# A hybrid attention and convolution layer on one core: low score products on half the array's rows, low weights last, and a new order

## The chip, the cores and the metric

The kernel runs on one core of a Trainium2 chip. The metric is the device time of one execution in microseconds (us). Of the kernel before, three runs were timed: a median of 910.27 us (909.42 to 910.80). One further execution was recorded by the profiler.

## What is computed

One layer on 1024 positions of width 1024: an RMS norm, one input projection to 5632 columns, then two branches, attention over 16 heads of 64 (4 key and value heads) in three dilations and a causal convolution of 31 taps, both gated; an output projection, a residual and a last RMS norm. Cut to what matters here:

```python
h = rmsnorm(x, norm_g[layer])
proj = jnp.einsum('bsd,de->bse', h, w_in[layer])
q, k, v, a_gate, c_val, c_glu, c_gate = jnp.split(proj, split_idx, axis=-1)
y_att = attention_branch(q, k, v, a_gate)      # scores: einsum of q and k per block, softmax, times v
y_conv = conv_branch(c_val, c_glu, c_gate, conv_w[layer], ...)
y = jnp.concatenate([y_att, y_conv], axis=-1)
x = x + jnp.einsum('bse,ed->bsd', y, w_out[layer])
```

All of it is float32.

## The kernel before

**Numbers in two parts.** TensorE takes float32r operands, so a float32 number is split into a high part (its rounding to float32r) and a low part (what is left). A projection then is three products: high weight by high input, high weight by low input, low weight by high input. In the input projection (`inproj`, L640) a column of 128 outputs over 512 positions is 8 chunks of the width times these three, 24 products of 512 columns into one bank of PSUM. The tiles are `wh` and `wl` (weights), `hhi` and `hlo` (input), `ps` (result). The raw weight comes by a DMA of SP (`raw`); ScalarE writes `wh` and a negated copy, and a DMA of GpSimd's queue adds `raw` to the copy, which makes `wl` (`split_dma`). The first two weights are split by ScalarE and VectorE without that DMA.

**Scores.** Heads work in pairs (`attend`, L793). The 128 rows of a head's query tile hold the high part in one half of the rows and the low part in the other; for the first head of a pair (j = 0) the high part is in rows 0 to 63, for the second in rows 64 to 127. A key tile `kdh` holds the high part of the keys in both halves, `kdl` the low part in both. One product of 128 rows with `kdh` thus gives (high + low query) by high key, and a second one with `kdl` adds (high + low query) by low key. For each pair there are 32 such couples of products, called units: 16 far ones (8 of 96 columns, 8 of 224, tiles `qf`, `sc_..far`) and 16 near ones (2 of 128, 14 of 256, tiles `qs`, `sc_..near`). `score` (L830) writes the products of two or four units into one of two banks `sc`, then VectorE reads each unit with an add and a minimum (`add_min`, L283), and ScalarE takes the exponential. The transposes `tp_*`, the products `on`, `of` with the values and the additions follow.

**The order.** Nothing is issued in the order in which it is written. Every operation is recorded with a cost in microseconds, and `Plan.order` makes one list by simulating the engines: it picks ready operations by priority, keeps the number of buffers of a kind within `LIMITS`, and takes the streams of work from `SECTIONS` (which projections stand beside which pair of heads: h convolution input, k, q, v, a and c gates). `TUNE` holds the priorities. `mm` (L216) gives the cost of products. Each engine then executes its part of the list strictly in that order, waiting where data are late.

Of the kernel before, what the change touches and what calls it, by code (L numbers as in the profile page):

```python
# [19 lines left out]
ND = D // P  # L20
# [14 lines left out]
LIMITS = {"x": 5, "raw": 2, "raw_oc": 1, "raw_oa": 2, "wh": 3, "wl": 3, "tab": 1, "e": 7, "pt": 4, "vs": 4, "vc":  # L35
          4, "turn": 2, "opsa": 2, "score": 2, "hc": 5, "c": 7, "t": 1, "g": 1, "gl": 7, "y": 2, "ag": 4, "cc": 5,
          "qs": 5, "qf": 4, "kdh": 9, "kdl": 5, "yc": 1, "ya": 2, "zc": 7, "za": 3}
# [6 lines left out]
TUNE = {"w": 225, "use": 260, "ln": 65, "att": 240, "conv": -15, "wo": 185, "woa": 20, "ap": 0, "wait": 0.2116}  # L44
SECTIONS = [("k0 q0 h1 v", 0), ("h2 a0 q1", 1), ("h3 a1 q2", 1), ("a2 q3 h4", 1), ("h5 k1 a3 q4", 1), ("h6 a4 q5",
            1), ("c0 h7 a5 q6 c1 q7", 1), ("a6 a7 c2 c3", 1), ("c4 c5", 1), ("c6 c7", 0)]
# [115 lines left out]
class Plan:  # L162
# [57 lines left out]
    def mm(self, calls):  # L220
# [3 lines left out]
        for out, a, b, start, stop in calls:  # L224
            outs.append(out)
            ins += [a, b]
            n = b.cols if start is not None else P
            slow = 4.0 if start is not None and b.buf.dtype == F32 else 1.0
            cost += max(n * slow / 2210.0, 0.06 if start is not None else 0.109)
# [233 lines left out]
def layer_kernel(tc, x, norm_g, w_in, conv_w, conv_b, ln_g, ln_b, w_out, fin_g, tab, out):  # L463
# [176 lines left out]
    def inproj(col, use, cuts=((0, 512), (0, 512))):  # L640
        wh, wl = load_w(col)
        for half in range(2):
            b = bank("mm", f"ps{col}_{half}")
            for n0, n1 in zip(cuts[half], cuts[half][1:]):
                if n0:
                    yield 0.5
                for c in range(ND):
                    pl.mm([(b[:, n0:n1], wh[:, c, :], hhi[half][:, c, n0:n1], c == 0, False),
                           (b[:, n0:n1], wh[:, c, :], hlo[half][:, c, n0:n1], False, False),
                           (b[:, n0:n1], wl[:, c, :], hhi[half][:, c, n0:n1], False, c == ND - 1)])  # L650
# [142 lines left out]
    def attend(p):  # L793
# [36 lines left out]
        def score(name, units):  # L830
            sc = bank("sc", f"sc{p}_{name}", "score")
            calls, outs, o = [], [], 0
            for q, keys, t, e, s, near in units:
                dst = sc[:, o:o + e.cols]
                to = dst.crossed() if near else dst
                calls += [(to, q, keys(kh), True, False), (to, q, keys(kl), False, True)]
                outs.append(dst)
                o += e.cols
            pl.mm(calls)
            for (q, keys, t, e, s, near), dst in zip(units, outs):  # L840
# [3 lines left out]
        for j in range(2):  # L844
            score(f"{j}far0", [far_unit(j, r, 0) for r in range(4)])
            for r in (0, 2):
                score(f"{j}far{r + 1}", [far_unit(j, r, 1), far_unit(j, r + 1, 1)])
            yield 3.0
# [4 lines left out]
        for j in range(2):  # L853
            for b in (0, 2, 4, 6):
# [304 lines left out]
```

## Time and profile before

| | |
|---|---|
| median of three runs | 910.27 us |
| profiled execution | 910.03 us |
| its span, first to last instruction | 908.2 us |
| TensorE products (PE) | 875.1 us busy, 4493 instructions |
| weight loads (PEld) | 731.2 us |
| VectorE (DVE) | 656.1 us |
| ScalarE (ACT) | 591.3 us |
| mean granted TensorE clock | 0.984 |

The span lies 1.8 us under the profiled execution's own time. Busy times of PE are those of a pipeline: one product's latency is counted, and products overlap, so the distance between two starts tells what a product costs. The trace of the profiled execution is asked by groups, by stretches and as a timeline.

### The profile page before, as it was taken

Reading aid. Unit: us, or ns where it says so; the run is one execution under the profiler, and the core shown is the slowest. Engines: PE = TensorE matmul, PEld = TensorE weight load, DVE = VectorE, ACT = ScalarE, POOL = GpSimd, SP = SyncE. Lnnn points to the kernel's source line nnn. Section 1 sums busy time; section 2 is a strip of 40 time slices with the busy share of each in tenths; the row PEclk is TensorE's granted clock in tenths of the full one; section 3 lists DMA queues with packets and bytes.
Section 4 is the critical chain, followed back from the end, with each engine's and each line's share of the span. In section 5 each row is a group of like instructions: output and inputs, shape, how many; then the busy total and the mean of one; then the engine's idle time right before and its main releaser. Section 6 shows DMA issues by size and latency. Waiting matters only on the chain. (4 is left out here: it accounts for less than half of the span.)

```text
span 908.2 us, 13036 instructions
## 1 busy us (share of the span) xinstructions
PE 875.1 (96%) x4493; PEld 731.2 (81%) x4493; DVE 656.1 (72%) x1506; ACT 591.3 (65%) x1392; POOL 53.3 (6%) x69
## 2 busy tenths in 40 slices
PE   8999999999999999999998998899999899999996
PEld 7888888878888888878886887688887678778885
DVE  5769995798699699989587658874659895615432
ACT  5777469387979889678786764795796754404111
POOL 0011001101010110100011000001000000000000
PEclk9999999999999999999999999699999999999999
DMA  7653306436353673464357323366765697758211
GB/s 259 186 119 67 96 3 140 93 91 144 70 118 59 163 165 83 93 135 101 96 128 173 70 70 92 73 152 132 206 201 194 186 372 255 252 177 239 93 47 47
DMA packets 104953, 123.53 MB, mean 136 GB/s; under 512 B 17941, under 2 KB 78357, under 8 KB 104888
## 3 DMA queue, kind: packets, MB, share of 16 engines
q1 hardware_dynamic: 97000, 94.40, 33.6%
q0 software_dynamic: 7888, 28.32, 17.2%
q8 instruction: 35, 0.57, 0.3%
q14 instruction: 30, 0.25, 0.1%
HBM read 65.35 MB, written 24.84 MB: 99 GB/s over the span
## 5 line engine op out<-in xcount | busy, mean ns | idle before, releaser
L236 PE MATMUL ps<-hhi,wh 128*128 128x512 f32 (+1 forms) x720 | 291.1, 404 | 0.2 <-ACT hhi L249 0.2
L236 PE MATMUL ps<-hhi,wl 128*128 128x512 f32 (+1 forms) x720 | 282.3, 392 | 6.1 <-DMA wl<-raw 4.8
L236 PE MATMUL ps<-hlo,wh 128*128 128x512 f32 (+1 forms) x720 | 281.8, 391 | 0.4 <-DVE hlo L264 0.3
L236 PEld LDWEIGHTS ps<-hhi,wl 128*128 128x128 f32 x720 | 136.6, 190 | 38.2 <-DMA wl<-raw 6.5
L236 PEld LDWEIGHTS ps<-hlo,wh 128*128 128x128 f32 x720 | 137.2, 191 | 23.8 <-DVE hlo L264 1.0
L236 PEld LDWEIGHTS ps<-hhi,wh 128*128 128x128 f32 x720 | 137.0, 190 | 23.0 <-issue 0.5
L251 ACT ACTIVATE e<-e,near 128x256 f32<-128x256 f32 (+1 forms) x256 | 115.0, 489 | 17.4 <-DVE near L264 11.5
L268 DVE SCALAR_TENSOR_TENSOR c<-t,taps,c 128x511 f32<-128x511 f32 (+14 forms) x120 | 88.5, 737 | 0.0
L268 DVE SCALAR_TENSOR_TENSOR c<-hc,taps,c 128x511 f32<-128x511 f32 (+14 forms) x120 | 88.2, 735 | 0.3
L268 DVE SCALAR_TENSOR_TENSOR t<-hc,taps,t 128x511 f32<-128x511 f32 (+6 forms) x112 | 82.6, 738 | 0.3 <-ACT t L251 0.2
L236 PE MATMUL opsc<-woc,yhc 128*128 128x512 f32 (+1 forms) x272 | 81.0, 381 | 0.0
L251 ACT ACTIVATE e<-e,far 128x96 f32<-128x96 f32 (+1 forms) x128 | 53.8, 423 | 25.9 <-DVE far L283 25.2
L297 POOL DMA_DIRECT2D wl<-raw x40 | 34.9, 873 | 414.2 <-ACT wl L251 315.5
L236 PEld LDWEIGHTS opsc<-woc,yhc 128*128 128x128 f32 x272 | 50.1, 188 | 10.7
L236 PE MATMUL opsc<-woc,ylc 128*128 128x512 f32 (+1 forms) x136 | 52.0, 383 | 1.4 <-DVE ylc L264 1.4
L251 ACT ACTIVATE fjunk<-zc 128x512 bf16<-128x512 f32 (+1 forms) x17 | 10.3, 606 | 62.2 <-DVE zc L264 62.2
L236 PE MATMUL opsa<-woah,yla 128*128 128x512 f32 x112 | 45.0, 402 | 2.6 <-DVE yla L264 2.6
L249 ACT CAST wh<-raw 128x1024 fp32r<-128x1024 f32 x44 | 46.0, 1046 | 0.4 <-DMA raw<-in_w_in 0.4
L236 PE MATMUL opsa<-woah,yha 128*128 128x512 f32 x112 | 45.6, 408 | 0.4 <-DVE cc L264 0.4
L236 PE MATMUL opsa<-woal,yha 128*128 128x512 f32 x112 | 45.1, 402 | 0.0
L251 ACT ACTIVATE e<-e,f 128x224 f32<-128x224 f32 (+1 forms) x128 | 45.0, 436 | 0.0
L249 ACT CAST qf<-qs 128x512 fp32r<-128x512 f32 x32 | 34.3, 1120 | 13.5 <-DVE qs L268 13.5
(176 smaller groups left out, 1525.2 us busy)
## 6 DMA issues: line engine op xcount, KB each, us to landing
raw<-in_w_in SPq DMA_DIRECT2D x44, 512.0 KB, 5.4
wl<-raw POOLq DMA_DIRECT2D x40, 512.0 KB, 4.7
x<-in_x SPq DMA_DIRECT2D x8, 512.0 KB, 10.2
tab<-in_tab SPq DMA_DIRECT2D x8, 512.0 KB, 3.8
c_dram<-c SPq DMA_DIRECT2D x8, 512.0 KB, 2.7
g_dram<-g SPq DMA_DIRECT2D x8, 512.0 KB, 3.1
raw_oa<-in_w_out SPq DMA_DIRECT2D x8, 512.0 KB, 5.1
raw_oc<-in_w_out SPq DMA_DIRECT2D x8, 512.0 KB, 7.9
```

The source lines that it names most:

```text
L236: nc.tensor.matmul(out.ap(), a.ap(), b.ap(), start=start, stop=stop)
L249: nc.scalar.copy(out.ap(), x.ap())
L251: nc.scalar.activation(out.ap(), x.ap(), func, **{k: ap_of(v) for k, v in kw.items()})
L268: lambda: self.nc.vector.scalar_tensor_tensor(out.ap(), a.ap(), ap_of(s), b.ap(), op0, op1),
L297: self.op("POOL", 1.0, lambda: self.nc.gpsimd.dma_start(ap_of(dst), x.ap(), accum_op=ALU.add), [dst], [x, dst])
```

## The change

It does four things.

1. `score` now takes both heads of a pair in one call and fills both `sc` banks. First come the products with `kdh` over 128 rows for both heads, then those with `kdl`, which read only the 64 rows with the high part of the query, the heads in turn. The product of low query by low key is left out by that.
2. In `inproj` the 16 products with `wh` come first, then the 8 with `wl`.
3. The planner counts a product of 64 rows at half its cost.
4. `LIMITS`, `TUNE` and `SECTIONS` have other values, so the whole order is made anew. The number of products is the same.

```diff
@@ -32,18 +32,18 @@
 
 
 
-LIMITS = {"x": 5, "raw": 2, "raw_oc": 1, "raw_oa": 2, "wh": 3, "wl": 3, "tab": 1, "e": 7, "pt": 4, "vs": 4, "vc":
+LIMITS = {"x": 5, "raw": 1, "raw_oc": 1, "raw_oa": 2, "wh": 3, "wl": 3, "tab": 2, "e": 7, "pt": 4, "vs": 4, "vc":
           4, "turn": 2, "opsa": 2, "score": 2, "hc": 5, "c": 7, "t": 1, "g": 1, "gl": 7, "y": 2, "ag": 4, "cc": 5,
-          "qs": 5, "qf": 4, "kdh": 9, "kdl": 5, "yc": 1, "ya": 2, "zc": 7, "za": 3}
+          "qs": 5, "qf": 4, "kdh": 9, "kdl": 6, "yc": 2, "ya": 2, "zc": 7, "za": 3}
 
 RESERVE = {"e": 7, "pt": 3}
 BANKS = {"mm": 3, "sc": 2, "tp": 2, "o": 1}
 WARM = 55
 LATE = C_CG + 6 * P
 MORE = (10, 12)
-TUNE = {"w": 225, "use": 260, "ln": 65, "att": 240, "conv": -15, "wo": 185, "woa": 20, "ap": 0, "wait": 0.2116}
-SECTIONS = [("k0 q0 h1 v", 0), ("h2 a0 q1", 1), ("h3 a1 q2", 1), ("a2 q3 h4", 1), ("h5 k1 a3 q4", 1), ("h6 a4 q5",
-            1), ("c0 h7 a5 q6 c1 q7", 1), ("a6 a7 c2 c3", 1), ("c4 c5", 1), ("c6 c7", 0)]
+TUNE = {"w": 195, "use": 240, "ln": 65, "att": 240, "conv": 5, "wo": 215, "woa": -20, "ap": 0, "wait": 0.2116}
+SECTIONS = [("k0 q0 h1 v", 0), ("h2 a0 q1", 1), ("h3 a1 q2 a2", 1), ("q3 h4", 1), ("h5 k1 a3 q4", 1), ("h6 a4 q5",
+            1), ("c0 h7 a5 q6", 1), ("c1 q7 a6 a7 c2 c3", 1), ("c4 c5", 1), ("c6 c7", 0)]
 
 
 def score_tables():
@@ -226,7 +226,8 @@
             ins += [a, b]
             n = b.cols if start is not None else P
             slow = 4.0 if start is not None and b.buf.dtype == F32 else 1.0
-            cost += max(n * slow / 2210.0, 0.06 if start is not None else 0.109)
+
+            cost += max(n * slow / 2210.0, 0.06 if start is not None else 0.109) * (0.5 if a.hi - a.lo == DH else 1.0)
 
         def fn():
             for out, a, b, start, stop in calls:
@@ -646,8 +647,10 @@
                     yield 0.5
                 for c in range(ND):
                     pl.mm([(b[:, n0:n1], wh[:, c, :], hhi[half][:, c, n0:n1], c == 0, False),
-                           (b[:, n0:n1], wh[:, c, :], hlo[half][:, c, n0:n1], False, False),
-                           (b[:, n0:n1], wl[:, c, :], hhi[half][:, c, n0:n1], False, c == ND - 1)])
+                           (b[:, n0:n1], wh[:, c, :], hlo[half][:, c, n0:n1], False, False)])
+                for c in range(0, ND, 2):
+                    pl.mm([(b[:, n0:n1], wl[:, c + i, :], hhi[half][:, c + i, n0:n1], False, c + i == ND - 1)
+                           for i in range(2)])
             pl.boost = TUNE["use"]
             use(half, b, slice(half * 512, half * 512 + 512))
             pl.boost = 0
@@ -828,32 +831,35 @@
                     sf[:, r, :, 2 * j + half:2 * j + half + 1], False)
 
         def score(name, units):
-            sc = bank("sc", f"sc{p}_{name}", "score")
-            calls, outs, o = [], [], 0
-            for q, keys, t, e, s, near in units:
-                dst = sc[:, o:o + e.cols]
-                to = dst.crossed() if near else dst
-                calls += [(to, q, keys(kh), True, False), (to, q, keys(kl), False, True)]
-                outs.append(dst)
-                o += e.cols
-            pl.mm(calls)
-            for (q, keys, t, e, s, near), dst in zip(units, outs):
+
+
+            first, second, todo = [], [[], []], []
+            for j in range(2):
+                sc, o = bank("sc", f"sc{p}_{name}_{j}", "score"), 0
+                for q, keys, t, e, s, near in units[j]:
+                    dst = sc[:, o:o + e.cols]
+                    to, r = dst.crossed() if near else dst, slice(j * DH, j * DH + DH)
+                    first.append((to, q, keys(kh), not o, False))
+                    second[j].append((to, q[r], keys(kl)[r], False, len(second[j]) == len(units[j]) - 1))
+                    todo.append((e, dst, t, s))
+                    o += e.cols
+            pl.mm(first + [c for both in zip(*second) for c in both])
+            for e, dst, t, s in todo:
                 pl.add_min(e, dst, t, 3e38, s[:, 0])
                 pl.act(e, e, AF.Exp, bias=s[:, 0], scale=-1.0, accum=s[:, 1])
 
-        for j in range(2):
-            score(f"{j}far0", [far_unit(j, r, 0) for r in range(4)])
-            for r in (0, 2):
-                score(f"{j}far{r + 1}", [far_unit(j, r, 1), far_unit(j, r + 1, 1)])
-            yield 3.0
+        score("far0", [[far_unit(j, r, 0) for r in range(4)] for j in range(2)])
+        yield 3.0
+        for r in (0, 2):
+            score(f"far{r + 1}", [[far_unit(j, r, 1), far_unit(j, r + 1, 1)] for j in range(2)])
+            yield 2.0
         there, back = (dram([512, n], f"{x}{p}") for x, n in (("there", 8), ("back", 4)))
         near_rows, far_rows = ("(b p) x -> p b x", dict(p=P)), ("(u r) x -> u r x", dict(r=4))
         pl.store(there.rows(far_rows[0], **far_rows[1]), sf.shaped("p a b c -> p a (b c)", 4, 8))
         pl.load(st[:, :, 1, :, :].shaped("p a b c -> p a (b c)", 4, 8), there.rows(near_rows[0], **near_rows[1]))
-        for j in range(2):
-            for b in (0, 2, 4, 6):
-                score(f"{j}near{b}", [near_unit(j, b), near_unit(j, b + 1)])
-                yield 1.0
+        for b in (0, 2, 4, 6):
+            score(f"near{b}", [[near_unit(j, b), near_unit(j, b + 1)] for j in range(2)])
+            yield 2.0
         w = pl.buf("sx", [P, 4, 2, 2, 4], F32, f"w{p}")
         f = pl.buf("sx", [P, 4, 2, 4], F32, f"f{p}")
         least, low = w[:, :, 0, 0, :], [st[:, :, k, 0, :] for k in range(2)]
```

The order on TensorE (PE), at the scores of the last but one pair of heads (`sc6`; 0 and 1 are its heads in `sc6_1far0` and `sc6_far3_0`, the number behind far or near is the block; `ps896` is the projection of the last pair's queries, `ps4736` one of the convolution gates). Before:

```order
L236 MATMUL ps896_1_5562<-hhi1_424,wh896_5265 128x512
L236 MATMUL ps896_1_5562<-hlo1_439,wh896_5265 128x512
L236 MATMUL ps896_1_5562<-hhi1_424,wl896_5275 128x512
L236 MATMUL sc6_1far0_5613<-kdh3_3677,qf13_5355 128x96
L236 MATMUL sc6_1far0_5613<-kdl3_3703,qf13_5355 128x96
...
L236 MATMUL sc6_1far1_5622<-kdh3_3677,qf13_5355 128x224
L236 MATMUL sc6_1far1_5622<-kdl3_3703,qf13_5355 128x224
...
L236 MATMUL sc6_1far3_5634<-kdh3_3677,qf13_5355 128x224
L236 MATMUL sc6_1far3_5634<-kdl3_3703,qf13_5355 128x224
...
L236 MATMUL sc6_0near0_5647<-kdh3_3677,qs12_5318 128x128
L236 MATMUL sc6_0near0_5647<-kdl3_3703,qs12_5318 128x128
```

Now, at the same pair:

```order
L237 MATMUL ps4736_1_5500<-hhi1_420,wh4736_5272 128x512
L237 MATMUL ps4736_1_5500<-hlo1_430,wh4736_5272 128x512
L237 MATMUL ps4736_1_5500<-hhi1_420,wl4736_5284 128x512 x6
L237 MATMUL sc6_far3_0_5559<-kdh3_3578,qf12_5410 128x224 x2
L237 MATMUL sc6_far3_1_5560<-kdh3_3578,qf13_5416 128x224 x2
L237 MATMUL sc6_far3_0_5559<-kdl3_3598,qf12_5410 128x224
L237 MATMUL sc6_far3_1_5560<-kdl3_3598,qf13_5416 128x224
...
L237 MATMUL ps4736_1_5500<-hhi1_420,wl4736_5284 128x512 x2
L237 MATMUL ps896_0_5575<-hhi0_232,wh896_5455 128x512
L237 MATMUL ps896_0_5575<-hlo0_236,wh896_5455 128x512
...
L237 MATMUL sc6_near0_0_5598<-kdh3_3578,qs12_5394 128x128
```

Before, the three products of a chunk stand together, and the groups of scores of this pair follow one another; now the low weights are at the end of a half projection, both heads' low products alternate, and projection products stand between any two groups of scores (8 at least, in 22 of 56 cases exactly 8, in 11 more about 10).

The order on SP, at the start of the program (`raw3584` and `raw2560` are the first two weights, `raw1024` and `raw0` the next). Before:

```order
L294 DMA raw3584_164<-in_w_in 128x8x128
L294 DMA x2_166<-in_x 128x1024
L294 DMA x3_168<-in_x 128x1024
L294 DMA raw2560_170<-in_w_in 128x8x128
L294 DMA x4_172<-in_x 128x1024
...
L294 DMA raw1024_264<-in_w_in 128x8x128
L294 DMA rows_177<-in_conv_b 1x1024
L294 DMA raw0_273<-in_w_in 128x8x128
L294 DMA rows_177<-in_ln_b 1x1024
L294 DMA x7_321<-in_x 128x1024
```

Now:

```order
L295 DMA raw3584_164<-in_w_in 128x8x128
L295 DMA x2_166<-in_x 128x1024
L295 DMA x3_168<-in_x 128x1024
L295 DMA x4_170<-in_x 128x1024
...
L295 DMA rows_172<-in_conv_b 1x1024
L295 DMA rows_172<-in_ln_b 1x1024
L295 DMA raw2560_273<-in_w_in 128x8x128
L295 DMA x7_322<-in_x 128x1024
L295 DMA raw1024_339<-in_w_in 128x8x128
```

The second weight has moved from SP's 7th transfer to its 14th, behind the two row loads; the third and fourth follow it.

## Rows read from the trace of the kernel before

**Rows 1.** The page: its head, and each engine's busy us, share and instructions.
```profile
span 908.2 us, 13036 instructions
...
PE 875.1 (96%) x4493; PEld 731.2 (81%) x4493; DVE 656.1 (72%) x1506; ACT 591.3 (65%) x1392; POOL 53.3 (6%) x69
```

**Rows 2.** TensorE's groups by form: shapes, count | busy us, mean ns | idle before, releaser.
```profile
L236 PE MATMUL ps<-hhi,wl 128*128 128x512 f32 x688 | 272.5, 396 | 4.8 <-DMA wl<-raw 4.8
...
L236 PE MATMUL ps<-hhi,wl 128*128 128x256 f32 x32 | 9.8, 306 | 1.3 <-DVE wl L264 1.3
```

**Rows 3.** Timeline of TensorE, a near group: start us, us, what, [idle before <-releaser].
```profile
117.29 0.28 PE L236 MATMUL sc_0near<-kdl,qs 128*128 128x256 f32 x1
117.41 0.28 PE L236 MATMUL sc_0near<-kdh,qs 128*128 128x256 f32 x1
```

**Rows 4.** Timeline of the weight loads (PEld) in a far group of 96 columns.
```profile
70.03 0.19 PEld L236 LDWEIGHTS sc_0far<-kdh,qf 128*128 128x128 f32 x1
70.14 0.19 PEld L236 LDWEIGHTS sc_0far<-kdl,qf 128*128 128x128 f32 x1
```

**Rows 5.** Timeline of TensorE around the products of 34 rows.
```profile
25.89 0.38 PE L234 MATMUL xT<-ident,x 128*128 128x128 f32 x2
...
26.20 0.68 PE L234 MATMUL par_ps<-ident,rows 34*128 34x34 f32 x8
...
26.66 0.22 PE L234 MATMUL par_ps<-ident,rows 34*128 34x34 f32 x1
26.82 0.38 PE L236 MATMUL ps<-hhi,wh 128*128 128x256 f32 x1
27.04 0.28 PE L236 MATMUL ps<-hlo,wh 128*128 128x256 f32 x1
```

**Rows 6.** Timeline of TensorE at its longest wait for a low weight.
```profile
487.65 0.39 PE L236 MATMUL ps<-hhi,wh 128*128 128x512 f32 x1
487.88 0.40 PE L236 MATMUL ps<-hlo,wh 128*128 128x512 f32 x1
492.34 0.50 PE L236 MATMUL ps<-hhi,wl 128*128 128x512 f32 x1 [4.06 <-DMA wl<-raw]
```

**Rows 7.** Stretches: length, busy us (count) of PE, PEld, DVE, ACT, POOL, clock, DMA, GB/s.
```profile
493.00:496.40 3.40, 3.40 (x10) 2.66 (x9) 0.99 (x2) 0.00 (x0) 0.00 (x0) 0.50 1.10 209
568.10:581.70 13.60, 9.86 (x34) 8.22 (x35) 10.94 (x45) 11.10 (x39) 0.89 (x1) 0.50 0.48 113
```

**Rows 8.** Timeline of TensorE at a bunch of score products.
```profile
564.26 0.27 PE L236 MATMUL sc_1far<-kdh,qf 128*128 128x224 f32 x1
564.37 0.28 PE L236 MATMUL sc_1far<-kdl,qf 128*128 128x224 f32 x1
569.14 0.56 PE L236 MATMUL sc_1far<-kdh,qf 128*128 128x224 f32 x1 [4.49 <-DVE far L283]
...
571.95 0.41 PE L236 MATMUL sc_0near<-kdl,qs 128*128 128x256 f32 x1
...
577.50 0.45 PE L236 MATMUL sc_1near<-kdh,qs 128*128 128x128 f32 x1
```

**Rows 9.** Timeline of VectorE in the same stretch.
```profile
569.00 0.74 DVE L268 SCALAR_TENSOR_TENSOR c<-hc,taps,c 128x505 f32<-128x505 f32 x1
569.66 0.74 DVE L268 SCALAR_TENSOR_TENSOR t<-hc,taps,t 128x505 f32<-128x505 f32 x1
...
572.40 0.29 DVE L283 CUSTOM_DVE_ANT_0 e<-sc_0near,tab 128x128 f32<-128x128 f32 x1 [0.48 <-PE sc_0near L236]
...
572.61 0.42 DVE L283 CUSTOM_DVE_ANT_0 e<-sc_0near,tab 128x256 f32<-128x256 f32 x1
...
572.96 0.74 DVE L268 SCALAR_TENSOR_TENSOR c<-hc,taps,c 128x504 f32<-128x504 f32 x1
```

**Rows 10.** Timeline of SP's DMA issues at the start, the two row loads.
```profile
10.58 7.88 SPq L294 DMA_DIRECT2D rows<-in_conv_b  x1
...
19.25 3.20 SPq L294 DMA_DIRECT2D rows<-in_ln_b  x1
```

## The prediction

> **What bounds the kernel now.** I read the head of the page first: TensorE is busy 96% of a span of 908.2 us, no other engine above 72% [rows 1]. So what counts is how long TensorE's queue of products takes and where it stands still. The groups by form give the bulk: 688 products of 512 columns with low weights and as many of each of the two other kinds, and the only DMA wait among them is 4.8 us before those with the low weights [rows 2]. "Mean ns" there is latency; what a product costs the queue is the distance between starts in the timeline: 0.23 us for 512 columns (487.65, 487.88) [rows 6], 0.12 us, more closely 0.115, for 256 [rows 3], 0.11 for 224 (564.26, 564.37) [rows 8]. One of 96 columns is no cheaper, because the weight loads, one before each product, come 0.11 us apart [rows 4]: short products are paced by their loads. Last I looked for stops: the largest are 4.06 us for a low weight [rows 6] and the stretch from 564 to 577 us, where score products follow one another without a projection between them [rows 8].
>
> The profiled execution took 910.03 us, 0.24 us under the median of 910.27; the sum is made against 910.03. A change of less than 0.2%, 1.8 us, can't be told from none here.
>
> **Part 1, the low score products.** Per pair of heads 32 products with the low part of the keys (14 near ones of 256 columns, 2 of 128, 8 far ones of 224, 8 of 96) now read 64 rows, two heads' products alternating between the halves of the array. Counting the two 128-column ones as 256, a pair of heads has 4 near groups, 2 far groups of 224 and one of 96; eight pairs make 32, 16 and 8 groups, 56 in all.
>
> What can be gained: if the two halves run side by side, each two products cost as one. That is 2 x 0.115 = 0.23 us per near group, 2 x 0.11 = 0.22 per far group, 4 x 0.11 = 0.44 per group of 96 columns: 7.4 + 3.5 + 3.5 = 14.4 us.
>
> What it costs: the array changes from 128 rows to 64 and back once per group. The trace has a place where it works on few rows, eight products of 34 rows, par_ps, amid products of 128 [rows 5]. Going in: the transposes xT start 0.11 us apart, the last at 26.00, so the next product could start at 26.11; it starts at 26.20, 0.09 later. Going out: par_ps's eight start 0.065 us apart (26.20 to 26.66), so the next could start at 26.72; it starts at 26.82, again 0.1 later, and the one behind it 0.22 us after that (27.04) where 0.12 is usual, as its weights could not be loaded ahead: 0.10 more. I take 0.19 us per change of rows, so 0.38 per group. The sum per near group is -0.23 + 0.38 = +0.15. For the far groups I count less, because products paced by loads pay part of it already: a 224-column one streams for about 0.10 of its 0.11 us, one of 96 for 0.04, so a far group gets +0.15 and a group of 96 -0.44 + 2 x 0.12 = -0.20. That makes 32 x 0.15 + 16 x 0.15 - 8 x 0.20 = **+5.6 us**.
>
> The bounds: with no change cost at all it is -14.4. With the full change cost and the two halves' loads one after the other at 0.11 us [rows 4], nothing is saved: +0.36 near, +0.37 far, +0.25 for 96 columns, 11.5 + 5.9 + 2.0 = +19.4. I take +5.6, because the change cost is seen on the way in and on the way out, and loads into separate halves need not wait for each other as loads into the same rows do; that last point no row shows.
>
> The Trainium skill, TensorE: Matmul & The Clock Gate, section "LDWEIGHTS (loading the stationary operand)", says that a load over 32 rows takes as long as over 128; taken together with loads in turn this would give the +19.4. The Trainium skill, TensorEngine Tiling (Array Packing), section "Theoretical Speedup", gives up to twofold for 64 rows or fewer, which alone would give the -14.4; its "Key Properties" say that tiles load and multiply in parallel but that a change of tiling mode drains the engine, which is on the side of the +5.6.
>
> **Part 2, low weights last.** In each half projection the first product with wl is now the 17th, not the 3rd: 14 x 0.23 = 3.2 us later. The 4.06 us stop [rows 6] shrinks to 0.85, the other 0.7 us of the 4.8 [rows 2] vanish: -3.9. The stop was followed by a stretch of 3.4 us (493.0 to 496.4) with TensorE fully busy at a granted clock of 0.50, its 1.2 GHz level [rows 7], which costs 1.7 us; without the stop I take it away. **-5.6 us**; bounds 0, if another load is late by more than 3.2 us, and -7.
>
> **Part 3, the start.** The limit of raw buffers falls from 2 to 1, so the second weight (raw_170 before, raw_273 now) moves from SP's 7th transfer to its 14th, with the two small row loads, which held SP for 7.88 and 3.20 us [rows 10], directly ahead. Its product can be late. Against this, the first low weight, for which TensorE waits 1.3 us [rows 2], is needed 14 products later. I take **0**, bounds -3 (that wait and its after-effect on the clock) and +4 (the second weight issued only when the last row load is through, at 22.45 as before [rows 10], and landing some us after, while the 24 products of 0.12 us and the transposes ahead of it end near 23).
>
> **Part 4, the order.** Before, the second head of one pair (sc_1far) and all its near groups stand on TensorE back to back. VectorE, busy with convolution pieces among other things, came to them late [rows 9], so TensorE stood 4.49 us before one group and shorter before others. From 564.48 to 577.50 it did 20 score products, 2.3 us of work, in 13.0 us: 10.7 lost [rows 8]. The clock was at 0.50 from 568.1 to 581.7 [rows 7]; the 4.2 us after 577.5 lose another 2.1. In the new order no score group follows another with fewer than 8 projection products (8 x 0.23 = 1.86 us) between, so this bunch is gone: **-12.8 us**.
>
> In its place: a group now fills both score banks, so the next one waits until VectorE has read all of them. Four near passes of 0.35 us each (starts 572.61 to 572.96) and 0.45 us from the last product's start (571.95) to the first pass (572.40) [rows 8, 9] make 1.85 us, just what 8 projection products cover. 22 of the 56 groups have only 8. A convolution piece under way (0.66 us from start to start, 569.00 to 569.66) adds some 0.3 us on average: 22 x 0.3 = **+6.6 us**. All other transfers and the out projection keep their work; I cost them at nothing, as TensorE covers them now and its queue there stands as before.
>
> The sum: 910.0 + 5.6 - 5.6 + 0 - 12.8 + 6.6 = **903.8 us**, predicted 904.
>
> **Rivals.**
> *The halves take turns.* Loads stay 0.11 us apart, so each low product keeps its price and the changes of rows come on top: 904 + (19.4 - 5.6) = 918 us, slower. For it: in every row short products are paced by loads. Against: all those loads go to the same rows. It decides if two low products of a pair start more than about 0.06 us apart.
> *VectorE holds both banks.* If each of the 33 groups with 10 or fewer projection products ahead (11 have about 10) meets a whole convolution piece of 0.66 us, 33 x 0.66 = 21.8 in place of 6.6: 919 us, slower. For it: the bunch showed such waits. Against: TensorE is busy 96% of the span [rows 1]. It decides from a mean wait of 0.53 us.
> *The change of rows is free.* Part 1 is -14.4: 884 us. Against it stand both delays around the 34 rows [rows 5].
> *The stop only moves.* New waits of the bunch's size appear elsewhere: about 910 to 916.
>
> **How the numbers follow.** The forecast has 0.42 (its own range 897 to 911), the halves in turn 0.22, both banks 0.12, the free change 0.12, the moved stop 0.12. The first gives faster 0.38, same 0.02, slower 0.02; in turn and both banks nearly all slower, with 0.04 faster should part 4 bring more; the free change all faster; the moved stop 0.03 faster, 0.06 same, 0.03 slower. Together faster 0.57, same 0.08, slower 0.35. The range 887 to 919 leaves out most of the free change and the upper tails of the two slower ones, 2 in 10.
>
> **What would show it.** Right: low score products of a pair starting within 0.03 us of each other; a gap of about 0.2 us ahead of the first low product and of the projection product behind; no wait for wl above 1 us; between 540 and 600 us a clock at 1.00 and no stop above 2 us. Wrong: low products 0.11 us apart; waits for VectorE before most score groups; a stop of several us near 23 us for the second weight.

## The result, and the profile after

The changed kernel takes 899.28 us (median of four, 898.14 to 904.34) against 910.53 us for the kernel before beside it: a ratio of 0.9889, 95% interval 0.9851 to 0.9928. It is faster by 11.3 us; the prediction was 904 us. The profiled execution is the fastest of the four (898.14 us); what the one of 904.34 us lost was not recorded.

The page of the changed kernel, its head and the engines, against [rows 1]:

```profile
span 896.3 us, 13046 instructions
...
PE 873.2 (97%) x4493; PEld 720.2 (80%) x4493; DVE 655.8 (73%) x1506; ACT 592.8 (66%) x1392; POOL 53.3 (6%) x69
```

The span is 11.9 us shorter, with as many products. Busy time can't tell where that came from; the idle time in the groups by form does (count | busy us, mean ns | idle before):

```profile
L237 PE MATMUL ps<-hhi,wl 128*128 128x512 f32 x688 | 184.2, 400 | 0.0
...
L237 PE MATMUL sc_near<-kdh,qs 128*128 128x256 f32 x112 | 19.9, 288 | 0.0
...
L237 PE MATMUL sc_near<-kdl,qs 64*128 64x256 f32 x112 | 14.7, 329 | 0.0
...
L237 PE MATMUL ps<-hhi,wl 128*128 128x256 f32 x32 | 4.4, 281 | 0.0
L237 PE MATMUL sc_near<-kdh,qs 128*128 128x128 f32 x16 | 4.0, 250 | 0.8 <-DVE far L284 0.5
```

The waits for low weights, 4.8 and 1.3 us [rows 2], are zero. All score groups together wait 0.8 us (11.1 before, most of it in the bunch of [rows 8]). The low score products now read 64 rows; their latency rose (329 ns), which says nothing of their price. The price is in the starts. TensorE's timeline at a near group and at a group of 96 columns:

```profile
128.39 0.40 PE L237 MATMUL ps<-hhi,wl 128*128 128x512 f32 x1
128.63 0.63 PE L237 MATMUL sc_near<-kdh,qs 128*128 128x256 f32 x4
129.19 0.50 PE L237 MATMUL sc_near<-kdl,qs 64*128 64x256 f32 x4
129.62 0.44 PE L235 MATMUL vT_f<-ident,vt 128*128 128x128 f32 x2
...
72.42 0.65 PE L237 MATMUL sc_far<-kdl,qf 64*128 64x96 f32 x8
73.00 0.51 PE L237 MATMUL ps<-hhi,wh 128*128 128x512 f32 x1
73.34 0.40 PE L237 MATMUL ps<-hlo,wh 128*128 128x512 f32 x1
```

In the first group the four high products start at 128.63, 128.74, 128.86 and 128.97, the low ones at 129.186 and 129.189, then 129.409 and 129.412: in pairs, 3 ns apart. From the last high start to the first low one it is 0.21 us, not 0.115; from pair to pair 0.22; from the last pair to the next product 0.21. So each pair is one, and the change of rows delays twice. On the way out the second projection product is late too: behind the second group it starts 0.34 us after the first (73.00, 73.34). But at this group most of that is old, 0.31 in the kernel before (70.74, 71.05 in its trace); it is the near groups where it is new, 0.34 in place of 0.23 (shown at e1).

Three stretches of the changed kernel, the one that answers to [rows 7] (540 to 600 us) and the two with a low clock that are longest outside the last microseconds:

```profile
540.00:600.00 60.00, 60.00 (x317) 49.40 (x315) 46.54 (x124) 52.92 (x130) 5.18 (x6) 1.00 0.52 122
22.70:26.10 3.40, 2.84 (x14) 2.44 (x13) 2.67 (x5) 2.78 (x7) 0.00 (x0) 0.50 0.75 217
698.50:708.70 10.20, 7.29 (x20) 5.72 (x21) 8.63 (x18) 8.90 (x13) 0.00 (x0) 0.50 0.91 282
```

TensorE is busy for all of the 60 us at a granted clock of 1.00, its 2.4 GHz level. The stretches at 0.50, the 1.2 GHz level, each begin around a stop. These are the largest stops left after the start, in TensorE's timeline (one of 1.19 us at 311.04 is left out):

```profile
21.54 0.66 PE L235 MATMUL par_ps<-ident,rows 34*128 34x34 f32 x8 [1.70 <-DMA rows<-in_ln_b]
...
695.17 1.02 PE L237 MATMUL var<-avg,ss 128*128 128x1 f32 x8 [1.23 <-DVE ss L265]
700.48 2.05 PE L237 MATMUL rb<-ident,lst 128*128 128x128 f32 x8 [4.28 <-DVE lst L269]
...
799.90 0.50 PE L237 MATMUL opsc<-woc,ylc 128*128 128x512 f32 x1 [1.45 <-DVE ylc L265]
```

The stop of 4.28 us for `lst` was 2.29 us before; the one of 1.45 us was there before too, with the same length. VectorE's timeline shows why the first grew: the splitting of output weights (`woal`, `woc`) now stands between the small steps `lst` that TensorE waits for, 2.41 us from the first step to the second (1.26 in the kernel before, 709.12 to 710.38, where those weights are split ahead of the first):

```profile
696.23 0.16 DVE L275 TENSOR_SCALAR lst<-var 128x4 f32<-128x4 f32 x1 [0.61 <-PE var L237]
696.31 1.22 DVE L265 TENSOR_TENSOR woal<-raw_oa,woah 128x1024 fp32r<-128x1024 f32 x1
697.44 1.29 DVE L265 TENSOR_TENSOR woc<-raw_oc,woc 128x512 fp32r<-128x512 f32 x2
698.64 0.17 DVE L280 RECIPROCAL lst<-lst 128x4 f32<-128x4 f32 x1
```

One account is used for all kernels below. *Idle* is the sum of TensorE's idle time ahead of its products. *Clock* is half of the time at a clock of 0.50, up to its last product, in which it was not idle. *Rest* is the span less both: the work itself, with the 7 us behind the last product. Median is that of the timed runs; the other columns are of the one profiled execution.

| kernel | low score rows | median us | span | idle | clock | rest |
|---|---|---|---|---|---|---|
| before | 128 | 910.5 | 908.2 | 26.0 | 11.8 | 870.5 |
| changed | 64 | 899.3 | 896.3 | 15.7 | 5.1 | 875.6 |
| e1, full rows, order kept | 128 | 894.6 | 899.6 | 20.5 | 9.0 | 870.1 |
| e2, more changes of rows | 64 | 923.0 | 921.3 | 15.4 | 6.5 | 899.4 |
| e3, same half | 64 | 914.2 | 916.6 | 18.6 | 9.0 | 889.0 |
| e4, low weight third, order kept | 64 | 933.9 | 933.4 | 40.6 | 16.7 | 876.2 |
| e5, change's code, old tables | 64 | 917.0 | 911.7 | 25.9 | 10.0 | 875.8 |
| e6, old code, change's tables | 128 | 895.5 | 892.9 | 14.5 | 5.1 | 873.4 |
| e7, full rows, order anew | 128 | 902.2 | 900.7 | 20.4 | 7.9 | 872.4 |
| e8, low weight third, order anew | 64 | 923.2 | 917.0 | 25.9 | 13.8 | 877.3 |
| e9, e6 and low weights last | 128 | 894.8 | 894.6 | 17.2 | 8.1 | 869.2 |
| e10, old code, SECTIONS alone | 128 | 921.1 | 919.1 | 30.0 | 17.7 | 871.4 |
| e11, old code, LIMITS alone | 128 | 914.2 | 913.2 | 28.5 | 10.2 | 874.5 |
| e12, old code, TUNE alone | 128 | 910.8 | 907.2 | 25.0 | 11.7 | 870.4 |

Between before and changed, idle and clock fall by 17.0 us (37.8 to 20.8) and the work grows by 5.1.

### The profile page after: what moved, and what is told of

The parts are those of the page before. It is cut to its first block, busy times and chain, and to the rows that moved or that the text cites. A ratio compares the mean times of both kernels' runs of the same rounds, so it can differ in the third digit from the quotient of the medians.

```text
span 896.3 us, 13046 instructions
## 1 busy us (share of the span) xinstructions
PE 873.2 (97%) x4493; PEld 720.2 (80%) x4493; DVE 655.8 (73%) x1506; ACT 592.8 (66%) x1392; POOL 53.3 (6%) x69
## 4 chain that ended last, share of the span: by engine, by line
PE 86%; DMA 7%; DVE 3%; ACT 2%; issue 1%; SPq 1%; POOL 0%; DVEq 0%; ACTq 0%; POOLq 0%
PE ps L237 52%; PE opsc L237 10%; PE opsa L237 7%; PE sc_near L237 3%; PE on L237 3%; PE of L237 3%; PE sc_far L237 2%; DMA y<-comb 2%; PE tp_p L235 1%; PE tp_m L235 1%; DMA rows<-in_ln_b 1%; PE tp_s L235 1%; DMA raw_oc<-in_w_out 1%; ACT e L252 1%; DMA yc<-yc_dram 1%; DMA x<-in_x 1%
## 5 line engine op out<-in xcount | busy, mean ns | idle before, releaser
L237 PE MATMUL ps<-hhi,wh 128*128 128x512 f32 (+1 forms) x720 | 288.1, 401 | 0.3 <-ACT hhi L250 0.2
L237 PE MATMUL ps<-hhi,wl 128*128 128x512 f32 (+1 forms) x720 | 188.7, 395 | 0.0
L237 PEld LDWEIGHTS ps<-hhi,wl 128*128 128x128 f32 x720 | 129.3, 188 | 27.9
L252 ACT ACTIVATE e<-e,far 128x224 f32<-128x224 f32 (+1 forms) x128 | 54.0, 424 | 36.0 <-DVE far L284 35.7
L284 DVE CUSTOM_DVE_ANT_0 e<-sc_near,tab 128x256 f32<-128x256 f32 (+1 forms) x128 | 45.0, 404 | 9.9 <-PE sc_near L237 9.2
L252 ACT ACTIVATE e<-e,f 128x96 f32<-128x96 f32 (+1 forms) x128 | 44.5, 439 | 0.2 <-DMA f<-back 0.2
```

Of the source, the lines that this page charges most:

```text
L237: nc.tensor.matmul(out.ap(), a.ap(), b.ap(), start=start, stop=stop)
L252: nc.scalar.activation(out.ap(), x.ap(), func, **{k: ap_of(v) for k, v in kw.items()})
L284: lambda: self.nc.vector.tensor_tensor_reduce(out.ap(), a.ap(), b.ap(), 1.0, ap_of(first), ALU.add, ALU.min, least.ap()),
```

## The experiments

The first four keep the changed kernel's place for every operation and change only what is issued there; the last eight let the planner order anew. "Tables" are the numbers in `LIMITS`, `TUNE` and `SECTIONS`.

### e1: the 64 rows undone, order kept

```diff
-            pl.mm(first + [c for both in zip(*second) for c in both])
+            full = [[], []]
+            for j in range(2):
+                for (to, q, k, a, b), (q0, k0) in zip(second[j], whole[j]):
+                    full[j].append((to, q0, k0, a, b))
+            pl.mm(first + [c for both in zip(*second) for c in both],
+                  emit=first + [c for both in zip(*full) for c in both])
```

`whole` holds the operands over all 128 rows; `emit` is what is issued in place of what is planned.

> The changed kernel with one part undone: the low score products read all 128 rows again; both heads in one call, low weights last and the order of every engine stay as they are. If a change of rows costs 0.38 us per group and the halves side by side gain 14.4 us in all, as the prediction's part 1 has it, this is 5.6 us faster than the changed kernel: about 893.7 us. If the halves' work is what made the change faster (free change of rows), it is up to 14 us slower than the changed kernel: about 913 us. If the score products do not bound the stretch they stand in, no difference: 899 us.

Measured: 894.56 us, ratio to before 0.9838 (0.9792 to 0.9884). Against the changed kernel 4.7 us faster, where the prediction priced part 1 at 5.6. Three of the four executions took 894.5 to 894.6 us; the fourth, 901.37, is the profiled one and stands in the table, with this stop, of which the changed kernel's trace has none:

```profile
633.21 0.50 PE L237 MATMUL sc_near<-kdh,qs 128*128 128x128 f32 x2 [3.88 <-DVE far L284]
```

The column of the work agrees with the medians: 871.5 us on average over the eight kernels with 128 rows (869.2 to 874.5), 876.2 over the four with opposite halves and one visit to 64 rows per group (changed, e4, e5, e8; 875.6 to 877.3). That is 4.7 us. The spread of 5 us among kernels with the same products is not explained; it is about how far the account can be trusted.

As the order is the same, each group can be set beside itself. A near group of the changed kernel and the same one in e1:

```profile
132.66 0.63 PE L237 MATMUL sc_near<-kdh,qs 128*128 128x256 f32 x4
133.22 0.50 PE L237 MATMUL sc_near<-kdl,qs 64*128 64x256 f32 x4
133.65 0.50 PE L237 MATMUL ps<-hhi,wh 128*128 128x512 f32 x1
133.99 0.40 PE L237 MATMUL ps<-hlo,wh 128*128 128x512 f32 x1
```

```profile
134.11 0.64 PE L237 MATMUL sc_near<-kdh,qs 128*128 128x256 f32 x4
134.59 0.64 PE L237 MATMUL sc_near<-kdl,qs 128*128 128x256 f32 x4
135.06 0.40 PE L237 MATMUL ps<-hhi,wh 128*128 128x512 f32 x1
135.30 0.40 PE L237 MATMUL ps<-hlo,wh 128*128 128x512 f32 x1
```

From its first product to the second projection product behind it, the group takes 1.33 us with halves and 1.19 with full rows. Counted to the third product behind, over the 53 groups that no stop and no low clock touches in either trace, the median difference is 0.16 us more with halves in near groups, 0.16 more in far groups of 224 and 0.18 less in groups of 96. Over all 56 groups that is about 6 us.

### e2: more changes of rows

Each unit's two high products are followed at once by its two low ones, 128 excursions to 64 rows in place of 56.

```diff
-            pl.mm(first + [c for both in zip(*second) for c in both])
+            a, b = first[:len(units[0])], first[len(units[0]):]
+            pl.mm(first + [c for both in zip(*second) for c in both],
+                  emit=[c for f0, f1, s0, s1 in zip(a, b, *second) for c in (f0, f1, s0, s1)])
```

> The changed kernel with the array's rows changed more often: within a group, each unit's two products of 128 rows are followed at once by its two of 64 rows, so that a group of two units changes rows there and back twice instead of once, one of four units four times. That is 48 + 8 x 3 = 72 more changes there and back. At 0.38 us each for groups of 224 and 256 columns and some 0.25 for 96 columns: 48 x 0.38 + 24 x 0.25 = 24 us more, about 923 us, if the product queue bounds these stretches. If the change of rows is hidden or free: 899 us.

Measured: 923.02 us, ratio 1.0125 (1.0084 to 1.0166). The work grows by 23.8 us (875.6 to 899.4) for 72 more excursions: 0.33 us each on average. TensorE's timeline in it:

```profile
128.72 0.50 PE L237 MATMUL sc_near<-kdh,qs 128*128 128x256 f32 x2
129.15 0.38 PE L237 MATMUL sc_near<-kdl,qs 64*128 64x256 f32 x2
129.46 0.50 PE L237 MATMUL ps<-hhi,wh 128*128 128x512 f32 x1
129.80 0.39 PE L237 MATMUL ps<-hlo,wh 128*128 128x512 f32 x1
```

Again 0.34 us in place of 0.23 at the second product after the low ones. The change of rows is not free. The 24 us expected were 48 visits at 0.38 and 24 at 0.25, the ones between 96-column products; 23.8 is what both prices together gave.

### e3: both heads in the same half

```diff
-                    to, r = dst.crossed() if near else dst, slice(j * DH, j * DH + DH)
+                    to, r = dst.crossed() if near else dst, slice(0, DH)
```

> The changed kernel with the second head's low products reading rows 0 to 63 like the first head's, instead of rows 64 to 127 (so the second head's scores take the low part of the query there). Order and number of products are the same. If the gain of 14.4 us comes from two products running in opposite halves at once, it is lost here, the loads taking turns: 13 to 14 us slower than the changed kernel, about 913 us, with starts of low products about 0.11 us apart. If two products of 64 rows overlap wherever they stand: 899 us.

Measured: 914.21 us, ratio 1.0046 (1.0022 to 1.0070). The same near group:

```profile
129.65 0.63 PE L237 MATMUL sc_near<-kdh,qs 128*128 128x256 f32 x4
130.21 0.73 PE L237 MATMUL sc_near<-kdl,qs 64*128 64x256 f32 x4
130.88 0.33 PE L235 MATMUL vT_f<-ident,vt 128*128 128x128 f32 x1
```

From the first low start to the next product it is 0.67 us, against 0.43 in the changed kernel (129.19 to 129.62). In one half the products take turns; only opposite halves run side by side. The work is 13.4 us more, close to the 14.4 that the prediction counted for side by side, and the time is 4 us under the 918 of that rival. The Trainium skill, TensorE: Matmul & The Clock Gate, "Part 3: Packing small matmuls — row/col tiling", says that products in different row groups start about 4 ns apart, and the 3 ns here agree. It also says that a weight load overlaps with running products only where the row groups differ. With that the traces do not agree: in the kernel before, a load for all 128 rows runs from 69.70 us for 0.19 us while a product of 512 columns over the same rows, started at 69.69, has the array until the next product at 69.92. What the same half prevents here is two products side by side.

### e4: the low weight third, order kept

```diff
+                left = [(wx, hx, c) for c in range(ND) for wx, hx in ((wh, hhi), (wh, hlo), (wl, hhi))]
+                if half or col >= LATE:
+                    left.sort(key=lambda r: r[0] is wl)
...
+                        i = next(i for i, r in enumerate(left) if r[0] is not wl or hasattr(wl.buf, "there"))
```

In the first half projection of a weight (all but the last two weights) the products are issued chunk by chunk, as before the change, at the places that the changed kernel has for them.

> The changed kernel with one part undone: in the first half projection of each weight (but the last two weights) the low weight's products stand third in each chunk again, as far as that low weight's DMA has been issued in the program by then; every other engine's order and every other product's place stay. In the trace of the changed kernel some 9 of 39 low weights land 1 to 8 us after the third product's start and before the 17th's, about 20 us in all. If low weights last is what hides these, this is 8 to 20 us slower, 907 to 919 us (less than the sum, because a stop puts off what comes after it), with waits for the low weight's DMA before projections. If the DMAs are no bound: 899 us.

Measured: 933.90 us, ratio 1.0238 (1.0191 to 1.0285), 34.6 us over the changed kernel and above the range expected. The waits are there, and their longest:

```profile
L237 PE MATMUL ps<-hhi,wl 128*128 128x512 f32 x688 | 230.1, 406 | 20.8 <-DMA wl<-raw 20.7
```

```profile
271.33 0.79 PE L237 MATMUL ps<-hhi,wl 128*128 128x512 f32 x1 [6.37 <-DMA wl<-raw]
```

In the changed kernel's trace nine of 39 low weights land after the start of the third product of their projection, by up to 8.5 us, and low weights last hides all of it. What the expectation missed is that idle time grew by 24.9 us and the clock's share by 11.6 more: the stops bring stretches at 0.50 with them, 44.4 us in all against 13.7, up to the last product. But the changed order was made for low weights that are needed late, so this is not what the edit is worth by itself. That is the question of e8 and e9.

### e5 and e6: code and tables exchanged

e5 has the change's code with the tables of before, e6 the code of before with the change's tables; no other line differs.

> The change's code (both heads' scores in one group, low products on 64 rows, low weights last, half cost for them) with the numbers of the kernel before in LIMITS, TUNE and SECTIONS, from which the whole order is made again. On TensorE's list 2 of 55 score groups then follow another with nothing between (32 of 111 in the kernel before, none of 55 in the changed one). Theory: the stops go because a group now holds both heads and is given room by the code; the tables do little: 899 to 906 us, the two pairs of neighbouring groups costing up to 2 us of wait and 1.7 us of half clock each, and no stop above 2 us elsewhere between 30 and 690 us. Rival: the tables bring the gain: 910 us or more, with stops for score banks or weights as in the kernel before.

> The code of the kernel before with the change's numbers in LIMITS, TUNE and SECTIONS, the order made again: low weights third, low score products over 128 rows, one head per score group. 29 of 111 groups follow another with nothing between. Theory that the code brings the gain: 905 to 920 us, with one or more stops of 2 us or longer for a low weight or for VectorE's reading of scores. Rival, the tables bring it: about 895 us, that is 899 less the 4.7 us that the 64 rows cost.

Measured: e5 916.97 us, ratio 1.0078 (1.0054 to 1.0101); e6 895.49 us, ratio 0.9848 (0.9813 to 0.9883). My theory, that the code brings the gain, fell in both; the rival holds:

| | tables of before | the change's tables |
|---|---|---|
| code of before | 910 | 895.5 |
| the change's code | 917.0 | 899.3 |

The tables are worth 14.5 and 17.7 us, the code costs 7.0 and 3.8. With the old tables, the new code stops again where low weights are last and score groups hold both heads:

```profile
472.90 0.50 PE L237 MATMUL ps<-hhi,wl 128*128 128x512 f32 x1 [4.38 <-DMA wl<-raw]
```

```profile
486.58 0.48 PE L237 MATMUL sc_far<-kdh,qf 128*128 128x224 f32 x2 [2.52 <-DVE far L284]
```

And with the new tables, the old code has neither stop, though its low weights are third and 29 of its 111 score groups follow another with nothing between; its score groups wait 4.2 us in all, 1.04 at most. The stretch of the bunch in e6:

```profile
540.00:600.00 60.00, 60.00 (x315) 50.58 (x314) 48.51 (x131) 51.87 (x134) 4.35 (x5) 1.00 0.45 108
```

and its groups by form, the 512-column products with low weights:

```profile
L236 PE MATMUL ps<-hhi,wl 128*128 128x512 f32 x688 | 271.4, 394 | 0.3 <-DMA wl<-raw 0.3
```

### e7 and e8: parts of the code undone, order anew

```diff
e7
-            cost += max(n * slow / 2210.0, 0.06 if start is not None else 0.109) * (0.5 if a.hi - a.lo == DH else 1.0)
+            cost += max(n * slow / 2210.0, 0.06 if start is not None else 0.109)
...
-                    second[j].append((to, q[r], keys(kl)[r], False, len(second[j]) == len(units[j]) - 1))
+                    second[j].append((to, q, keys(kl), False, len(second[j]) == len(units[j]) - 1))
e8
-                           (b[:, n0:n1], wh[:, c, :], hlo[half][:, c, n0:n1], False, False)])
-                for c in range(0, ND, 2):
-                    pl.mm([(b[:, n0:n1], wl[:, c + i, :], hhi[half][:, c + i, n0:n1], False, c + i == ND - 1)
-                           for i in range(2)])
+                           (b[:, n0:n1], wh[:, c, :], hlo[half][:, c, n0:n1], False, False),
+                           (b[:, n0:n1], wl[:, c, :], hhi[half][:, c, n0:n1], False, c == ND - 1)])
```

> The changed kernel with low score products over all 128 rows, counted by the planner at their whole cost, so that the order is made again with the change's tables (the run with full rows kept the order of the changed kernel). 55 groups, one with less than 1 us of projection ahead. Theory: 892 to 898 us, like the 894.6 with the order kept, since what counts is the full rows and the spaced groups. Rival: that order was a lucky one of many, a new one brings stops of its own: 900 to 910 us.

> The changed kernel with the low weight third in each projection again, as in the kernel before, and the order made again for that (the run with the low weight third kept the changed kernel's order and took 933.9 us). Theory: a late low weight is what low weights last protect from, and the planner cannot foresee all of it: 903 to 912 us, waits for wl of 3 to 8 us in all, each long one with 3.4 us of half clock behind it, and up to 3 stops at the score groups that now stand together. Rival: the planner puts the loads early enough: 899 us, no wait for wl above 1 us. Second rival: all the waits of the run with the order kept remain: 930 us or more.

Measured: e7 902.23 us, ratio 0.9921 (0.9892 to 0.9951); e8 923.15 us, ratio 1.0145 (1.0104 to 1.0185). e7 issues the same products as e1 and takes 7.7 us more: only the order differs. It has waits of 1.7 and 2.1 us that e1 has not, though the two traces can't be set against each other whole, as e1's is of its slowest execution. The longer one:

```profile
343.23 0.50 PE L237 MATMUL ps<-hhi,wl 128*128 128x512 f32 x1 [2.06 <-DMA wl<-raw]
```

e8 lies above the theory's range. Its stops of over 2 us are one for a low weight (2.14), but also one for transposed scores (2.35, at 606.37) and two at the end (2.89 and 2.18); with the others it has 19.0 us more of idle and clock than the changed kernel. Of its 10.2 us of new idle time 2.3 are waits for a low weight's DMA; the rest the new order brought elsewhere, so e8 doesn't price low weights last.

### e9: low weights last alone, with the change's tables

The edit is e8's in reverse, on e6.

> The kernel before with the change's tables (895.5 us by itself) and the low weights last in each projection, the order made again; scores as before. Waits for low weights in the run without this edit are 0.3 us in all, so by the theory that only stops count it can give nothing directly: 893 to 900 us, the rest being what another order does. Rival, the prediction's step 2: 5.6 us faster, 890 us or less. Second rival: it is this edit, not the 64 rows, by which the change's code is slower with the same tables: 899 us or more, with new stops.

Measured: 894.75 us, ratio 0.9837 (0.9812 to 0.9862), within 0.8 us of e6. Where the order leaves no wait for a low weight, moving the low weights gives nothing and costs nothing that these executions (891.7 to 896.4 us) tell from none. So the 3.8 us that the change's code costs with its tables are hardly from this part.

### e10 to e12: one table at a time

Each is the kernel before with one of the three tables of the change.

> The kernel before with the change's SECTIONS alone. The bunch of score products at 564 to 577 us and the wait for a low weight at 492 us lie beside the section whose list the change cuts in two. Theory: the gain of the tables (14.5 us with the code of before) is mostly here: 896 to 902 us, no stop above 2 us between 480 and 600 us. Rival: the gain comes only with all numbers together: 907 us or more, with stops elsewhere.

> The kernel before with the change's LIMITS alone (one raw buffer in place of two, two for tab and yc, six for kdl). The prediction's step 3 has 0 for the start, between -3 and +4. Theory: 907 to 914 us, the stops at 492 and 564 to 577 us or others of their size still there. Rival: buffers decide where those stops are: 902 us or less.

> The kernel before with the change's TUNE alone (priorities of weights, of what uses a projection, of the convolution and of the out projection's weights). Theory: convolution pieces held VectorE ahead of the bunch, and conv goes from -15 to 5, so a part of the gain may be here: 902 to 910 us. Rival: all of the tables' gain, 897 us or less. If the three parts do not add up to 14.5 us, each order has stops of its own and the numbers have no separate worth.

Measured: SECTIONS alone 921.12 us, ratio 1.0134 (1.0117 to 1.0151); LIMITS alone 914.17 us, 1.0055 (1.0040 to 1.0070); TUNE alone 910.76 us, 1.0010 (0.9994 to 1.0025). The kernel before beside them took 909.29. One by one they make it 11.8, 4.9 and 1.5 us slower, the last not clear of none; together they make it 14.5 us faster. The theory for SECTIONS fell: the bunch has moved to 469 us and grown. In its trace the wait for a low weight is back at another place, and ahead of the moved bunch there is one for ScalarE:

```profile
469.10 0.55 PE L236 MATMUL sc_0far<-kdh,qf 128*128 128x224 f32 x1 [3.13 <-ACT qf L249]
```

```profile
637.68 0.80 PE L236 MATMUL ps<-hhi,wl 128*128 128x512 f32 x1 [4.51 <-DMA wl<-raw]
```

With LIMITS alone the bunch of [rows 8] stays, and so it does with TUNE alone, a line each:

```profile
568.25 0.56 PE L236 MATMUL sc_1far<-kdh,qf 128*128 128x224 f32 x1 [4.72 <-DVE far L283]
```

```profile
568.88 0.56 PE L236 MATMUL sc_1far<-kdh,qf 128*128 128x224 f32 x1 [4.53 <-DVE far L283]
```

The eight kernels with 128 rows do 869 to 874.5 us of work. They differ mainly by what idle and clock add, from 20 to 48 us.

The fastest are e1 (894.56), e9 (894.75) and e6 (895.49), which these runs don't tell apart. All beat both kernels, and all have full rows and the change's tables.

## Why the prediction was right, and where it was not

**What bounds it.** Right: TensorE's queue and its stops. The work of the products changed by 5.1 us, the stops and the clock by 17.0.

**Part 1, the low score products.** Right in sign, mechanism and size: +5.6 predicted, 4.7 measured by the medians with the order kept, about 6 group by group, and each kind of group within 0.02 us of its +0.15, +0.15 and -0.20 (e1). Both halves of the sum hold by themselves: side by side is worth 13.4 of the 14.4 us (e3), and 72 more visits to 64 rows cost 23.8 of the 24 us (e2). The row of eight small products amid large ones [rows 5] gave the price, with some luck: the `par_ps` products are transposes, and behind transposes of all 128 rows the second product is late as well, here 0.20 us after the first, with no change of rows:

```profile
22.10 0.60 PE L234 MATMUL xT<-ident,x 128*128 128x128 f32 x4
22.46 0.36 PE L236 MATMUL ps<-hhi,wh 128*128 128x256 f32 x1
22.66 0.28 PE L236 MATMUL ps<-hlo,wh 128*128 128x256 f32 x1
```

So that row alone could not show the last 0.10 of the price; the near groups do. The Trainium skill, TensorEngine Tiling (Array Packing), "Key Properties", has the drain on a change of mode but no price for it. Here four low products side by side save less than a visit costs, so the 48 groups with four lose 0.16 us each, and the 8 groups with eight gain 0.18.

**Part 2, low weights last.** The 4.8 us of waits went, and the half-speed stretch at 493 us with them. That this edit is the cause is not shown: with the new tables the waits are 0.3 us with low weights third (e6), and last gives nothing more (e9). The changed order does lean on it, as e4 shows. -5.6 was right as a sum of what went (idle and clock between 480 and 500 us fall from 5.8 us to 0), but that it is the price of the edit is not shown.

**Part 3, the start.** 0 was taken, between -3 and +4. There is no stop for the second weight; TensorE waits 1.70 us for the row load and 0.56 for a transpose, in place of 1.35 us for the first low weight, with one stretch of 3.4 us at half speed as before; in idle and clock the first 30 us cost 0.6 us more. The two row loads, which had held SP for 7.88 and 3.20 us [rows 10], take 0.24 us each at their new place. The first pair's scores begin 1.6 us later (71.51 in place of 69.92 us), which also has to do with what is ahead of them.

**Part 4, the order.** The bunch at 564 to 577 us is gone and the clock there is 1.00, as forecast: -12.8, and 12.1 us of idle and clock went between 560 and 585. The reason given, 8 projection products between any two groups, is more than is needed: e6 has pairs of groups back to back there and no stop. The traces show what the orders with the stop have in common, a long run of groups with nothing between: 8 in the kernel before (7.2 us idle in that run), 8 in e11 (7.4) and e12 (7.2), 10 in e10 (6.9, at 469 us, 3.1 of it for ScalarE); e6 has 4 at most (1.2 us idle), e9 and the changed kernel 2, counted by the head. No run changes that length alone, so that it is the cause is argued. One table does not break the long run up (e10 to e12); two at a time were not run, and which of the tables' numbers do it stays open.

**The mis-sized term** is the "+6.6" for VectorE holding both banks. All score groups together wait 0.8 us: only four products of them by more than 0.1 us, where 22 groups were expected to wait 0.3 on average. VectorE is busy 46.54 of 60 us between 540 and 600 and still in time. This is more than the 4.7 us between 904 and 899. But 0.8 us is what one execution shows, the fastest. e1 to e4 have the same order, and their score groups wait 5.3, 0.3, 3.3 and 4.2 us, most of it in three of them (3.88, 3.13 and 3.94) at one and the same group, where the changed kernel waits little:

```profile
631.64 0.50 PE L237 MATMUL sc_near<-kdh,qs 128*128 128x128 f32 x2 [0.39 <-DVE far L284]
```

So VectorE can be late there, at one group and not at 22; whether it was in the execution of 904.34 us is not known.

**What the sum left out** is the small score waits ahead of 480 us, where idle time fell by 2.1 us, and the end. There the wait for `lst` grew from 2.29 to 4.28 us, one of 1.23 us came ahead of it, and the half-speed stretch grew from 3.4 to 10.2 us; before, another stop of 2.18 us at 775 us, with a stretch of 3.4 us behind it, went. In idle and clock the end costs 2.0 us more (12.2 from 680 us on, 10.1 before from 690 on). The prediction costed the out projection "at nothing", as its queue there "stands as before"; VectorE's did not. So in part "the stop only moves" was true.

**The rivals.** *The halves take turns*: no, 3 ns apart; e3 shows what it would have been. *VectorE holds both banks*: no, 0.8 us, and at most 5.3 in the kernels with the same order, against 21.8. *The change of rows is free*: no, e1 and e2. *The stop only moves*: in the changed kernel in small; in e5, e8 and e10 nearly wholly (25.9, 25.9 and 30.0 us of idle time, 26.0 before).

## What to carry to other kernels

Before using half of the array, count the products per visit: two that run side by side save one, and each visit costs about 0.38 us here, 0.25 among products of 96 columns. With four low products in most visits the kernel lost 4.7 us.

Where one planner makes the whole order, an edit and the order it brings must be measured apart: issue the edit in the old order's places once, and exchange the tables once. Eight kernels with nearly the same work ran from 894.6 to 921.1 us mainly by their stops and the clock behind them, so a difference of 10 us between two orders says little of the edit that caused it.

Price a stop with the stretch at the lower clock behind it, and look for the new stops on the engine that the moved work shares, here VectorE at the end.

## What the runs showed of the hardware

Two products on opposite halves of the rows start 3 ns apart (129.186 and 129.189). Two on the same half take turns (e3). From the first of four to the next product it is 0.43 us in the one case and 0.67 in the other.

A change between 128 and 64 rows delays the first product by about 0.1 us on the way in and on the way out (0.21 us from start to start in place of 0.12 at the near group of 128.63), and the second one behind each by about 0.1 us more (0.22 for 0.12 on the way in, 0.34 for 0.23 on the way out).

The stops of over 2 us shown here each have a stretch at a granted clock of 0.50 that begins during them (698.5 us in the changed kernel, in the stop up to 700.48) or soon behind them (493.0 in the kernel before, after 492.34). It lasted 3.4 us there, with TensorE busy for all of it, and 13.6 at the bunch of score products [rows 7]. In e4 this added 11.6 us to the 24.9 us of new idle time.
